# Two diffusion layers on one core: 32 products of the tile of ones by itself on TensorE, ahead of the first sums of squares

## The chip, the core and the metric

The kernel runs on one core of a Trainium2 chip. The metric is the time of one execution on the device, in microseconds (us). The engines are named as in the profile: PE is TensorE's matmul and PEld its weight load, DVE is VectorE, ACT is ScalarE, POOL is GpSimd, SP is SyncE, which here only issues DMAs.

## What is computed

Two layers of a diffusion transformer over 512 latent tokens and 256 context tokens with 1024 features, all in float32. Each layer normalises its input (root mean square), scales and shifts it by vectors made from a conditioning vector, runs attention, projects, and runs a SwiGLU feed-forward part. The part that matters here is the very beginning of layer 0:

```python
silu_c = jax.nn.silu(c)[:, None, :]
sh_a, sc_a, ... = jnp.split(silu_c @ mod_w[l] + mod_b[l], 6, axis=-1)
a_lat = rms_norm(h_lat) * (1 + sc_a) + sh_a      # modulate
p_lat = a_lat @ w_in
```

The output is the final normalisation of the latent stream, 512 by 1024.

## The kernel before, in words

Tokens lie along the free dimension and features along the 128 partitions, so x is eight tiles `X[k]` of 128 features by 512 latent and 256 context tokens. The tile `ones` (128 by 128, float32, all 1.0) is filled by DVE in line 177; it is the operand that sums over partitions.

The first stage runs as follows (lines 867 to 912).

- Lines 161 to 163 load the latent columns of the eight `X[k]`, half from SP's queue and half from POOL's.
- Lines 871 to 874 square each tile on ACT (`square_sum`, line 363) and add the squares on DVE (line 366) into one tile, `acc`.
- `first_norm` (line 796) sums `acc` over the partitions with four products by one column of `ones` (line 801), takes the root on ACT (line 803), the reciprocal on DVE (line 804) and makes a diagonal tile of it on DVE (line 805).
- `chunk(1, 0)` (line 815) makes a quarter of the scale vector: eight products of the conditioning vector by weights that SP's queue has loaded (line 823). `norm_spread` (line 809) spreads the reciprocal roots over the partitions with one product by `ones` (line 811) and copies the result into `r` (line 813). `chunk(0, 0)` makes the first quarter of the shift vector.
- `chunk_put` (line 827) copies such a quarter out (line 829), turns it with two small products (line 830) and adds the bias on DVE (line 835).
- Then `modulate` (line 409) makes `A[k]` on DVE (414), ACT (415) and DVE (416), and `start_products` (line 862) multiplies each `A[k]` by the value weights, which are loaded, cast and split on ACT and DVE in `load_start` (lines 848 and 849). Each such product is made of three (lines 757 to 759). `latent(k)` calls it for four token tiles, `context(k)` for two.

Three things set the order of the work. All products of this first stage are chained: `run` makes each group of products follow the last, so PE does them as they are written. The banks for the results come from `PM()`, which takes the PSUM tags `o` and `t` in turn; the four other tags of the first stage are held by the running sums `ov`. And the order on every engine is planned when the kernel is built: `SCHED` asks for a planner that gives each engine, at each time of a modelled run, the ready instruction with the best priority. Priorities follow the written order, and helpers shift some of them (`shifted`, for background work that makes the later scale and shift vectors, and for weights of later stages).

```python
def PM():
    turn[0] += 1
    return PS("ot"[turn[0] % 2])

def run(first, last):
    behind(first, *tip)
    tip[:] = [last]
```

After the first stage (from about 60 us on) come the projections, two attention parts, the output projection and the feed-forward part of layer 0, and the same for layer 1.

Of the kernel before, what the change touches and what calls it, by code (L numbers as in the profile page):

```python
# [14 lines left out]
P = 128  # L15
# [53 lines left out]
PATTERN = ("fbsfbsfbbsfs",) * 3  # L69
BG = ((0, 0, 0, 0, 0), (2, 3), (0, 0), (0, 0))  # L70
FIRST = 2000
STEPS = ((2, 3, 4, 4), 5, 3)
HALVES = (slice(0, 256), slice(256, 512))
SWAP8 = [(i // 16) * 16 + (i % 16 + 8) % 16 for i in range(32)]
# [24 lines left out]
def hybrid_kernel(ctx: ExitStack, tc, I, out):  # L99
# [6 lines left out]
    def T(tag, shape, dt=F32):  # L106
        count[0] += 1
        if tag not in SIZES:
            return sb.tile(shape, dt, tag=tag, name=f"{tag}_{count[0]}", bufs=BUFS.get(tag, 1))
        n = int(np.prod(shape[1:]))  # L110
        t = sb.tile([P, SIZES[tag] // (2 if dt == mybir.dt.bfloat16 else 4)], dt, tag=tag, name=f"{tag}_{count[0]}",
                    bufs=BUFS[tag])[: shape[0], :n]
        if len(shape) == 3:
            t = t.rearrange("p (a b) -> p a b", a=shape[1])
        return t
# [4 lines left out]
    def PS(tag):  # L120
        count[0] += 1
        return ps.tile([P, 512], F32, tag=tag, name=f"ps{tag}_{count[0]}", bufs=PBUFS[tag])
# [8 lines left out]
    V, S, G, PE = nc.vector, nc.scalar, nc.gpsimd, nc.tensor  # L131
# [9 lines left out]
    def behind(ins, *before):  # L141

        for x in before:
            tc.add_manual_dep(ins.ins, x.ins.name, mybir.DependencyInfo(mybir.DependencyClass.NoSync,
                              mybir.DependencyReason.DATA), reason="products in one run")
        return ins
# [29 lines left out]
    ones = T("ones", [P, P])  # L176
# [350 lines left out]
    def weighted(o, lanes):  # L527
# [13 lines left out]
        for n in range(max(len(m) for m in moving)):  # L541
            for i, (v, _, all_qs) in [*enumerate(lanes)][::-1]:
                if n < len(moving[i]):
                    kt, qs, t = moving[i][-1 - n]
                    c = slice((qs[0] - all_qs[0]) * P, (qs[-1] + 1 - all_qs[0]) * P)
                    with shifted(-FIRST):
                        ins = PE.matmul(o[64 * i : 64 * i + 64, c], v(kt), t, start=n == 0, stop=n == len(moving[i]) - 1)  # L547
# [97 lines left out]
    @contextmanager  # L645
    def shifted(by):
        tc.cur_priority += by
        yield
        tc.cur_priority -= by
# [21 lines left out]
    def attend(jobs, lag=LAG):  # L671

        todo = deque()
        outs[1] = PS("o") if PBUFS["o"] == 1 else None
        for j in jobs:
            n, units = rate[0]
            bg(int(len_jobs[0] * units) - int((len_jobs[0] - 1) * units))
            len_jobs[0] += 1
            pattern = PATTERN[phase[0]]
            sides, back, front = pattern.count("s"), todo.popleft() if len(todo) >= lag else None, True  # L680
            i = 0
            for x in pattern:
                if x == "s":
                    step((i + 1) * n // sides - i * n // sides)
                    i += 1
                elif x == "f":
                    front = front and next(j)
                elif back:
                    back = None if next(back, back) is back else back
            while front:  # L690
                front = next(j)
            if back:
                for _ in back:
                    pass
            todo.append(j)
        for j in todo:
            for _ in j:
                pass
# [88 lines left out]
# [3 lines that stand above are left out]
# [3 lines left out]
# [4 lines that stand above are left out]
# [70 lines left out]
    for comp in (0, 1):  # L867
        for v in range(2):
            MOD[0, comp, v] = T(f"mod0{comp}{v}", [P, 8])
    acc = None  # L870
    for k in range(KT):
        acc = square_sum(acc, X[k], LATS)
# [39 lines left out]
    def beside(gen):  # L912
        side_work.append(gen)
        return gen
# [80 lines left out]
    def split_pair(p):  # L995

        tag = ("b", "st")[p - 2]
        q, k = raws[2 * p - 4 : 2 * p - 2]
        how = S.copy, G.tensor_copy, V.tensor_copy
        sets.append((new_q(tag), new_k(tag)))  # L1000
        put_q(sets[p][0], None, how[RQ[p - 2]], (G, V)[RL[p - 2]])(q, slice(0, NT))
        yield
        put_k(sets[p][1], KC[1], how[RK[p - 2]])(k, slice(0, NT))
        yield
# [63 lines left out]
    def latent_operands(h):  # L1068
        p, s = divmod(h, 2)
        r, u = NOPE[s], USED[s]  # L1070
        rr = slice(32 * (h % 4), 32 * (h % 4) + 32)
        if p < 2:
            if p == 0:
                KA.append([T("st", [P, NT], F32R) for _ in range(2)])
            QA[s].append([T("st", [P, NT], F32R) for _ in range(2)])
            for t in [*(KA[s] if p == 0 else ()), *QA[s][p]] if s else ():
                (V if "z" in EV else G).memset(f(t[:32]), 0.0)
            if p == 0:
                for i in range(2):
                    V.tensor_copy(KA[s][i][ROPE[s]], KR[i][:32])  # L1080
        (ka, kc), (qa, qb) = KA[s], QA[s][p % 2]
        for x, (hi, lo) in ((kn[p], (ka, kc)), (qn[p], (qa, qb))):
            S.copy(hi[r], x[r])
            (V if "l" in EV and p < 1 else G).tensor_tensor(lo[r], x[r], f(hi[r]), op=ALU.subtract)
        for t, x in zip((qa, qb), QR[h // 4]):
            if "d" in EV:
                dma(t[ROPE[s]], x[rr])
            else:
                G.dma_start(t[ROPE[s]], x[rr])

        def scores(o, q, keys):
            q = slice(q * P, (q + 1) * P)
            PE.matmul(o, qa[u, q], ka[u, keys], start=True, stop=False)
            PE.matmul(o, qb[u, q], ka[u, keys], start=False, stop=False)
            PE.matmul(o, qa[u, q], kc[u, keys], start=False, stop=True)

        return scores
# [12 lines left out]
    def na_jobs():  # L1110
        for p in range(4):
            if p == 3:
                lower[0] = L3
            for x in ORDER[p]:
                beside(split_pair(int(x)) if x in "23" else {"n": latent_norms, "m": mla_prepare}[x]())
            rate[0] = STEPS[0][p], BG[0][p]
            if p % 2 == 0:
# [12 lines left out]
    i = 0  # L1130
# [21 lines left out]
    def mla_jobs():  # L1152
        phase[0], lower[0] = 1, LOWER
        rate[0] = STEPS[1], BG[0][4]
        ready.append(latent_operands(1))
# [392 lines left out]
    def swa_jobs():  # L1548
        for p in range(8):
            kv = p // 4  # L1550
            po = B()
            sums, mins = T("sm", [P, 6, 2]), T("sm", [P, 6, 2])
            hs = [Head(s, stacked_scores(sets[p][s], KS[kv]), keys_of(VS, kv), span, swa_bias,
                       sink_neg[:, 2 * p + s : 2 * p + s + 1], sums, mins) for s in range(2)]
            yield from pair_jobs(hs, po, False, swa_finish(p, po, sums, mins))
            OS.append(po)
# [9 lines left out]
    lower[0] = LOWER  # L1566
    rate[0] = STEPS[2], 0
    attend(swa_jobs())
# [132 lines left out]
```

## Time and profile before

| what | value |
|---|---|
| median of 3 runs | 1612.67 us (1612.62 to 1614.48) |
| the profiled execution | 1610.99 us |
| its span, from first to last instruction | 1609.1 us |
| mean granted TensorE clock | 0.988 of full speed |
| first product on PE | 14.26 us after the start of the span |
| first product of the value projection (line 757) | 24.68 us |

Times inside the trace count from the start of the span. A view of the timeline gives start, length, engine, line, operation, output and inputs, how many records are merged, and in brackets the idle time ahead and what ended it. A view by windows gives for each stretch the busy time of the engines (with the number of records), the granted clock of TensorE, the busy share of the DMA engines and GB/s. A float32 product whose operands are plain float32 shows as two records, since line 811 issues one product and has two. The lengths of neighbouring records overlap, so the pace of PE is read from the distance of the starts.

### The profile page before, as it was taken

What the parts mean: (1) busy time and instruction counts of PE and PEld (TensorE: products, weight loads), DVE (VectorE), ACT (ScalarE), POOL (GpSimd) and SP (SyncE); (2) the same over time, 40 slices, a digit from 0 to 9 for tenths busy, and PEclk for the clock granted to TensorE, in tenths of its full rate; (3) what the DMA queues carried; (4) which work ended last, traced back from release to release, by engine and by line L of the source; (5) the groups of instructions that cost most, each with busy time, mean ns of one, the idle gap of its engine ahead of it and who ended that gap; (6) DMA issues with size and microseconds to landing.
All of it is one profiled execution on the core that took longest, in us unless ns stands there. A gap on an engine that the chain in (4) does not pass through costs nothing. (4 is left out here: it accounts for less than half of the span.)

```text
span 1609.1 us, 26559 instructions
## 1 busy us (share of the span) xinstructions
PE 1541.6 (96%) x9990; PEld 1371.1 (85%) x9990; DVE 1183.8 (74%) x2380; ACT 799.0 (50%) x1616; POOL 298.6 (19%) x324
## 2 busy tenths in 40 slices
PE   5989989999999999999999998999999999999997
PEld 3777867776899999998989896877779899899997
DVE  4773878668577678796867686779877688687685
ACT  4452587677365334342423244467756544354453
POOL 0231734230011111102021212384002000000002
PEclk9999999999999999999999998999999999999999
DMA  9634232102453455536456655132005133223322
GB/s 330 226 115 157 70 122 78 40 9 74 165 200 102 152 198 182 203 121 261 170 195 214 235 206 222 66 93 77 2 17 187 38 114 126 86 99 125 87 93 84
DMA packets 76536, 214.91 MB, mean 134 GB/s; under 512 B 10196, under 2 KB 17752, under 8 KB 76408
## 3 DMA queue, kind: packets, MB, share of 16 engines
q1 hardware_dynamic: 57432, 141.67, 26.4%
q0 software_dynamic: 16240, 68.30, 12.1%
q10 hardware_dynamic: 2736, 3.26, 0.6%
q8 instruction: 78, 1.28, 0.3%
q14 instruction: 50, 0.41, 0.1%
HBM read 186.97 MB, written 23.07 MB: 131 GB/s over the span
## 5 line engine op out<-in xcount | busy, mean ns | idle before, releaser
L318 ACT CAST wh<-wr 128x1024 fp32r<-128x1024 f32 (+2 forms) x148 | 114.8, 789 | 203.8 <-DMA wr<-in_w_dn_dram 35.4
L319 DVE TENSOR_TENSOR wl<-wr,wh 128x1024 fp32r<-128x1024 f32 (+2 forms) x145 | 135.1, 938 | 84.6 <-ACT wh L318 80.7
L553 ACT ACTIVATE p<-p,sm 128x512 f32<-128x512 f32 (+3 forms) x144 | 105.0, 730 | 32.4 <-DVE sm L557 30.5
L366 POOL TENSOR_TENSOR p<-p,p 128x256 f32<-128x256 f32 (+1 forms) x33 | 31.7, 960 | 468.5 <-PE psd L332 340.2
L1342 PE MATMUL pss<-b,wh 128*128 128x384 f32 (+1 forms) x344 | 107.0, 312 | 0.6 <-ACT b L355 0.6
L1343 PE MATMUL pss<-b,wh 128*128 128x384 f32 (+1 forms) x344 | 107.2, 312 | 0.1
L227 DVE CUSTOM_DVE_ANT_0 p<-rope,cond 128x1024 bf16<-128x1024 f32 x64 | 77.3, 1224 | 40.8 <-DMA rope<-in_mod_w_dram 40.5
L1344 PE MATMUL pss<-b,wl 128*128 128x384 f32 (+1 forms) x344 | 106.1, 312 | 0.0
L331 PE MATMUL psd<-b,wh 128*128 128x512 f32 (+3 forms) x256 | 88.2, 345 | 0.0
L329 PE MATMUL psd<-b,wh 128*128 128x512 f32 (+3 forms) x216 | 78.4, 363 | 2.9 <-ACT b L493 2.5
L547 PE MATMUL pso<-ph,b 128*64 128x256 f32 (+1 forms) x384 | 77.6, 360 | 2.1 <-DVE ph L492 2.1
L332 PE MATMUL psd<-b,wl 128*128 128x512 f32 (+3 forms) x216 | 77.1, 357 | 0.1
L547 PE MATMUL pso<-pl,b 128*64 128x256 f32 (+1 forms) x384 | 76.9, 359 | 0.2 <-DVE pl L492 0.2
L222 POOL DMA_DIRECT2D rope<-in_mod_w_dram x48 | 25.5, 531 | 244.1 <-DVE mod L227 229.3
L1344 PE MATMUL pst<-b,wl 128*128 128x384 f32 (+1 forms) x224 | 69.9, 312 | 0.0
L1343 PE MATMUL pst<-b,wh 128*128 128x384 f32 (+1 forms) x224 | 69.8, 312 | 0.0
L1342 PE MATMUL pst<-b,wh 128*128 128x384 f32 (+1 forms) x224 | 69.8, 312 | 0.0
L329 PE MATMUL pss<-st,wh 128*128 128x512 f32 (+2 forms) x200 | 68.2, 341 | 1.3 <-ACT st L1144 0.9
L331 PE MATMUL pss<-b,wh 128*128 128x256 f32 (+3 forms) x211 | 68.5, 325 | 0.1
L332 PE MATMUL pss<-st,wl 128*128 128x512 f32 (+2 forms) x200 | 68.0, 341 | 0.1
L1342 PEld LDWEIGHTS pss<-b,wh 128*128 128x128 f32 x344 | 65.2, 190 | 1.1 <-ACT b L355 0.9
L1343 PEld LDWEIGHTS pss<-b,wh 128*128 128x128 f32 x344 | 65.3, 190 | 0.9 <-DVE b L356 0.7
(674 smaller groups left out, 5423.8 us busy)
## 6 DMA issues: line engine op xcount, KB each, us to landing
wr<-in_w_gu_dram SPq DMA_DIRECT2D x88, 512.0 KB, 4.0
rope<-in_mod_w_dram POOLq DMA_DIRECT2D x48, 512.0 KB, 3.8
wr<-in_w_out_dram SPq DMA_DIRECT2D x32, 512.0 KB, 3.7
wr<-in_w_dn_dram SPq DMA_DIRECT2D x64, 256.0 KB, 2.8
p<-home POOLq DMA_DIRECT2D x40, 384.0 KB, 5.6
home<-p POOLq DMA_DIRECT2D x40, 384.0 KB, 5.0
wr<-in_w_in_dram SPq DMA_DIRECT2D x21, 512.0 KB, 3.9
nb<-in_nb_dram SPq DMA_DIRECT2D x16, 384.0 KB, 3.0
```

The source lines that it names most:

```text
L227: V.tensor_tensor_reduce(out=T("p", [P, D], mybir.dt.bfloat16), in0=w, in1=cond[:, v, :], op0=ALU.mult, op1=ALU.add, scale=1.0, scalar=0.0 ...
L318: behind(S.copy(h, r), *after[:1])
L319: behind((G if eng else V).tensor_tensor(lo, r, f(h), op=ALU.subtract), *after[1:])
L329: ins = PE.matmul(o, wh[:, k], mh[:, c], start=first and k == 0, stop=False)
L331: PE.matmul(o, wh[:, k], ml[:, c], start=False, stop=False)
L332: PE.matmul(o, wl[:, k], mh[:, c], start=False, stop=last and k == n - 1)
L366: marks["add"] = (eng or V).tensor_tensor(acc[:, :n], acc[:, :n], t[:, :n], op=ALU.add)
L547: ins = PE.matmul(o[64 * i : 64 * i + 64, c], v(kt), t, start=n == 0, stop=n == len(moving[i]) - 1)
L553: S.activation(p[:, c], p[:, c], AF.Exp, bias=nm, scale=-1.0, accum_out=dn)
L1342: PE.matmul(o, wh, xh, start=first and k == 0, stop=False, skip_group_check=not first)
L1343: PE.matmul(o, wh, xl, start=False, stop=False, skip_group_check=not first)
L1344: PE.matmul(o, wl, xh, start=False, stop=k == 3, skip_group_check=not first)
```

## The change

A constant `WARM = 32`, and ahead of the first squares, one more bank from `PM()` and 32 products of `ones` by `ones` into its first 128 columns, chained by `run`. Nothing reads their result.

```diff
+WARM = 32
...
     for comp in (0, 1):
         for v in range(2):
             MOD[0, comp, v] = T(f"mod0{comp}{v}", [P, 8])
+    d = PM()
+    for i in range(WARM):
+        ins = PE.matmul(d[:, :P], ones, ones, start=True, stop=True)
+        run(ins, ins)
     acc = None
     for k in range(KT):
         acc = square_sum(acc, X[k], LATS)
```

Since `PM()` is called once more, every later bank of the first stage that came from `t` now comes from `o`, and the other way round. Since `run` chains them, the four products of line 801 follow all 32.

## The prediction

> **What bounds the kernel now.** I read the page first, then the first 25 us in order of time, then PE's busy time and clock in equal stretches.
>
> ```profile
> span 1609.1 us, 26559 instructions
> ...
> PE 1541.6 (96%) x9990; PEld 1371.1 (85%) x9990; DVE 1183.8 (74%) x2380; ACT 799.0 (50%) x1616; POOL 298.6 (19%) x324
> ```
>
> PE is busy for 96% of the span, so over the whole the kernel is bound by PE. The change lies in the one place where PE has nothing to do: the start.
>
> ```profile
> 0.89 0.17 DVE L177 MEMSET ones<- 128x128 f32 x1
> ...
> 8.73 5.47 DVE L366 TENSOR_TENSOR p<-p,p 128x512 f32<-128x512 f32 x7 [7.68 <-ACT p L363]
> ...
> 14.25 1.78 PEld L801 LDWEIGHTS pst<-ones,p 128*128 128x128 f32 x8 [14.25 <-DVE p L366]
> 14.26 1.87 PE L801 MATMUL pst<-ones,p 128*128 128x1 f32 x8 [14.26 <-DVE p L366]
> ...
> 16.05 1.93 PE L823 MATMUL pso<-st,cond_col 128*32 128x256 f32 x16
> ...
> 16.67 0.69 DVE L805 TENSOR_TENSOR p<-ident_r,sm 128x512 f32<-128x512 f32 x1
> ...
> 17.92 2.08 PE L811 MATMUL pst<-p,ones 128*128 128x512 f32 x2
> ...
> 20.35 0.64 PE L823 MATMUL pso<-ph,cond_col 128*32 128x256 f32 x2
> ...
> 20.78 0.55 PE L823 MATMUL pso<-ph,cond_col 128*32 128x256 f32 x2
> ...
> 21.16 0.38 PE L823 MATMUL pso<-ph,cond_col 128*32 128x256 f32 x2
> ...
> 22.08 0.61 PE L830 MATMUL pso<-pick,p 128*128 128x2 f32 x4
> ...
> 22.39 1.42 DVE L414 SCALAR_TENSOR_TENSOR p<-b,mod,nb 128x512 f32<-128x512 f32 x2
> ...
> 24.68 0.80 PE L757 MATMUL pss<-wh,b 128*128 128x512 f32 x1 [2.00 <-ACT b L415]
> ```
>
> PE waits 14.26 us, until DVE has added the last square at 14.20. DVE waits for the squares, and these for x, whose loads fill the DMA engines:
>
> ```profile
> 10.00:15.00 5.00, 0.74 (x4) 0.75 (x4) 3.68 (x6) 3.59 (x6) 0.00 (x0) 1.00 1.05 387
> ```
>
> A DMA share of 1.05 at 387 GB/s says that x can't come sooner, whatever PE does. From 14.26 to 22 PE itself is on the path: sums, scale quarter, spread, shift quarter, turn, then `modulate`, then the first real product at 24.68. The same operations run faster later on:
>
> ```profile
> 30.01 0.39 PE L823 MATMUL pso<-ph,cond_col 128*32 128x256 f32 x2
> ...
> 30.23 0.39 PE L823 MATMUL pso<-ph,cond_col 128*32 128x256 f32 x2
> ```
>
> ```profile
> 38.02 0.50 PE L801 MATMUL pst<-ones,p 128*128 128x1 f32 x4
> ...
> 44.10 0.59 PE L811 MATMUL pso<-p,ones 128*128 128x256 f32 x2
> ```
>
> Starts of line 823 are 0.43 us apart at 20.35 and 0.22 at 30.01. So PE runs at half speed until about 21, although the clock column of the windows says 1.00 there: it knows of no clock before the first change that it records. What changes the clock is read from PE's windows (busy us, records, clock, DMA share, GB/s), cut where the changes fall, 3.41 us each:
>
> ```profile
> 10.87:14.28 3.41, 0.02 (x1) 1.00 1.05 387
> 14.28:17.69 3.41, 3.41 (x24) 1.00 1.05 386
> 17.69:21.11 3.42, 3.42 (x18) 1.00 1.07 358
> 21.11:24.52 3.41, 1.57 (x16) 1.00 1.03 335
> 24.52:27.93 3.41, 3.25 (x8) 0.50 1.04 373
> 27.93:31.35 3.42, 3.42 (x40) 1.00 1.05 400
> ...
> 45.00:48.41 3.41, 1.34 (x5) 1.00 1.00 399
> 48.41:51.83 3.42, 3.42 (x10) 0.50 1.05 395
> ...
> 79.13:82.55 3.42, 0.34 (x2) 1.00 0.23 77
> 82.55:85.96 3.41, 2.90 (x13) 0.50 0.22 77
> 85.96:89.37 3.41, 2.06 (x15) 1.00 0.53 167
> 89.37:92.79 3.42, 1.17 (x5) 1.00 0.79 291
> 92.79:96.20 3.41, 3.41 (x10) 0.50 0.53 161
> ```
>
> The reader is to see a rule with no exception among these rows: a window in which PE was busy for 1.57 us or less is followed by one at exactly 0.50, one with 2.06 or more by one at 1.00. The early rows fit the same cuts: the speed changes between 20.78 and 21.16, at the cut 21.11. The window from 14.28, busy all along, did not raise the clock; it holds the sums, which stream one column each, and the narrow products of line 823, so busy time there isn't streaming.
>
> **The change part by part.** *Added: 32 products, two records each, 64 records.* They can start when `ones` is filled, at 0.89 + 0.17 = 1.06; I take 1.2. For the pace no row shows this product, but the nearest bound it closely. At half speed line 801 loads 8 weights in 1.78 us, 0.22 each, and line 811 streams 512 columns twice in 2.08 us: its second record is 1.22 us long, so the starts are 0.86 apart, or 0.215 for 128 columns. Load and stream of neighbours overlap in all these rows, so 0.215 a record. At full speed:
>
> ```profile
> 1089.11 0.93 PE L501 MATMUL psd<-ident_r,p 128*128 128x128 f32 x7
> ```
>
> The last of seven is 0.27 long, so (0.93 - 0.27) / 6 = 0.11 us. With the cuts of this trace (0.63, 4.04, 7.45, 10.87) the window to 4.04 is busy for 2.84 us, nearly the 2.90 that raised the clock at 85.96. Then (4.04 - 1.2) / 0.215 = 13.2 records run at half speed and 50.8 x 0.11 = 5.6 us follow: the products end at 9.6. If the clock rises only at 7.45, 29.1 records are slow and 34.9 x 0.11 = 3.8 us follow: they end at 11.3. If it never rises, 1.2 + 64 x 0.215 = 15.0.
>
> *What this does to the sums.* In the first two cases PE is free again 2.9 to 4.6 us ahead of 14.26, so the 32 cost the path nothing; DVE's chain to 14.20 is the cover. In the third the sums start 0.7 us late. And the clock: in the first case the window 10.87 to 14.28 holds no product, in the second 0.4 us, both far under 1.57. So the clock falls to half at 14.28, 0.02 us after the sums begin, and everything from there runs as before. **The gain on these cuts is nothing.**
>
> In another execution the cuts may lie otherwise; one trace cannot tell. The best place: products end at 11.3, a window that holds the last 2.06 us of them closes at 11.3 - 2.06 + 3.41 = 12.65 and keeps the clock, and the next closes at 16.06. The sums then run at full speed: 8 x 0.50 / 4 = 1.0 us instead of 1.87, 0.87 gained, and the scale quarter for the most part, so that the spread starts when the diagonal is ready, at 17.36 - 0.87 = 16.5 instead of 17.92: 1.4 gained at most. So between 0 and -1.4 us; I take -0.5.
>
> The Trainium skill (TensorE: Matmul & The Clock Gate, Seeing it yourself) prints a run in which the clock fell back 5.2 us after the last product. By that it would fall here at 9.6 + 5.2 = 14.8, and the first 0.6 us of sums would run fast, 0.3 gained, 1612.4; this trace speaks against so long a grace, as the clock fell at 24.52, under 2 us after line 830 ended at 22.08 + 0.61 = 22.69.
>
> *Moved: the banks.* `o` and `t` change places for the whole stage. `t` has two buffers, one of which is held, so both give one bank, used in turn at the same distance as before. Nothing; bounds 0.4 us either way, the 0.37 to 0.39 us of one small step.
>
> *The order on the other engines.* It is planned from modelled durations, and 32 products and a shifted clock are new to the plan. No row prices that; its ends are the rivals below.
>
> *Sum.* The profiled execution took 1610.99, its span 1609.1 and 1.9 around it; the median lies 1.7 above it. 1612.67 - 0.5 = **1612.2**. A measurement of this kernel tells about 0.2%, 3.2 us, from no change, so this is within it.
>
> **The rivals.** *1: the full clock holds (faster).* If PE still runs fast at 14.26 and on, the path shrinks: sums -0.87; spread starts 1.4 earlier in all, as above, and takes 2 x 0.59 - 0.1 = 1.1 instead of 2.08, so -2.4; the shift quarter takes 1.06 (30.01 to its last end) instead of 1.6, so -3.0. The first real product then starts near 21.7, the window to 24.52 holds 2.8 us of products, and the half window from 24.52 is spared: another 3.41 / 2 = 1.7. Together -4.7: **1608.0**. For it: the early steps all lie on the path, and after 27.93 PE is busy without a break. Against it: the empty window ahead of 14.28. It needs products that last at least to about 13, or a clock that stays up longer than at 24.52. What it may lose again is a late weight, since the DMA share is 1.03 to 1.07 up to 31 us.
>
> *2: the plan is redrawn for the worse (slower).* The place is 60 to 100 us:
>
> ```profile
> 60.00:80.00 20.00, 19.47 (x86) 15.77 (x84) 19.21 (x37) 11.11 (x22) 11.38 (x7) 1.00 0.38 129
> 80.00:100.00 20.00, 13.35 (x61) 11.53 (x62) 19.78 (x53) 12.00 (x35) 13.70 (x9) 0.83 0.44 147
> ```
>
> ```profile
> 83.06 0.55 PE L329 MATMUL pss<-b,wh 128*128 128x256 f32 x1 [3.59 <-DVE mod L253]
> ```
>
> DVE is full (19.21 and 19.78 of 20) and PE waits on it, 3.59 us at once. DVE instructions that PE needs and background ones for scale and shift vectors share that queue. Each background one (a row of line 227 gives 1.22 us) that the new plan puts ahead costs PE its length:
>
> ```profile
> L227 DVE CUSTOM_DVE_ANT_0 p<-rope,cond 128x1024 bf16<-128x1024 f32 x64 | 77.3, 1224 | 40.8 <-DMA rope<-in_mod_w_dram 40.5
> ```
>
> From three on (3.7 us) it decides. I price it at five, 6.1 us: **1618.7**. For it: the plan is one chain of choices by modelled time. Against it: if the model too has PE idle before the first sums, nothing after them moves and the order stays. The same lottery can gain as well, by about as much; a smaller chance, as PE has only 4% to win and DVE's full stretch everything to lose.
>
> *3: load and stream do not overlap.* Then a record takes 0.22 + 0.215 = 0.435 at half speed and about 0.22 at full, and the products end at 16.7 to 18.4. The sums start 2.4 to 4.1 late, but at full clock, worth -3.0: between -0.6 and +1.1, **1612.9**, again within 0.2%. L501's row, where each record has its own load and still comes every 0.11, speaks against it.
>
> **How the numbers follow.** The forecast, clock falls back and the order holds nearly: 0.39, with rival 3 at 0.04, both within 0.2%. Rival 1: 0.16, and a plan redrawn for the better: 0.08. Rival 2: 0.33. So faster 0.24, same 0.43, slower 0.33. The time is that of the likeliest, 1612.2. For 8 in 10 the range takes in rival 1 with a part of the better plans (1606.5) and most of rival 2, to about six instructions of 1.22 us (1620.0). Alone, the likeliest case reaches from 1610.9 (-1.4 and the banks) to 1613.8 (0.7 late and the banks).
>
> **What will show it.** The new line's 64 records should start by 1.3, come every 0.215 us, then every 0.11, and end between 9.5 and 11.5. The first clock change on record should be a fall close to 14.3, and the starts of line 823 near 20 us should again be 0.43 apart. The first product of line 757 (renumbered) should start within 1.4 us of 24.68. If it starts near 21.7, rival 1 is right. If the first 60 us look alike and the idle times of PE between 79 and 99 have grown, or the lines come in another order, it is rival 2. A last product after 14.3 would break the pace that I assumed.

## The result, and the profile after

| | before | changed |
|---|---|---|
| median | 1612.67 us (7 runs, 1610.09 to 1615.73) | 1618.85 us (7 runs, 1615.72 to 1621.31) |
| ratio | | 1.0038, 95% interval 1.0022 to 1.0053 |
| the profiled execution, its span, its mean clock | 1610.99, 1609.1, 0.988 | 1615.72, 1613.9, 0.982 |

The changed kernel is slower by 0.38%, some 6 us. The forecast was 1612.2, no change that can be told; the price of rival 2, 1618.7, is what came.

From the page of the changed kernel, the span and the busy time of each engine:

```profile
span 1613.9 us, 26686 instructions
...
PE 1554.7 (96%) x10054; PEld 1385.0 (86%) x10054; DVE 1182.6 (73%) x2380; ACT 799.3 (50%) x1616; POOL 300.0 (19%) x324
```

PE has 64 more records, as counted, and 13.1 us more of busy time. The new products hold 9.1 of these (next view). So the 9990 old records take 4.0 us longer than before, although they are the same products. The windows below put this down to time at half clock. PE's idle time is 59.2 instead of 67.5. At the start 9.4 us of idle went (14.26 before; 1.10 and 3.78 now), so elsewhere there is 1.1 us more. 4.0 and 1.1 make 5.1, and the span grew by 4.8. What is lost is thus clock more than waiting.

The first 25 us of PE in order of time (start, length, and in brackets the idle time ahead and what ended it):

```profile
1.10 9.10 PE L873 MATMUL pst<-ones 128*128 128x128 f32 x64 [1.10 <-DVE ones L178]
13.98 1.05 PE L802 MATMUL pso<-ones,p 128*128 128x1 f32 x8 [3.78 <-DVE p L367]
...
16.83 1.85 PE L812 MATMUL pso<-p,ones 128*128 128x512 f32 x2
18.62 0.41 PE L824 MATMUL pst<-ph,cond_col 128*32 128x256 f32 x2
...
22.82 0.79 PE L758 MATMUL pss<-wh,b 128*128 128x512 f32 x1 [2.01 <-ACT b L416]
```

The products end at 10.2. The sums take 1.05 instead of 1.87, and the first real product starts 1.86 earlier than before, at 22.82 instead of 24.68. The start is better. The windows of this execution, cut at its own clock changes (busy us with records, clock, DMA share, GB/s), show why:

```profile
8.09:11.51 3.42, 2.12 (x19) 1.00 1.04 397
11.51:14.92 3.41, 0.94 (x8) 1.00 1.05 387
14.92:18.33 3.41, 3.41 (x20) 0.50 1.05 384
18.33:21.75 3.42, 2.48 (x25) 1.00 0.93 297
21.75:25.16 3.41, 2.34 (x6) 0.50 0.87 267
25.16:28.57 3.41, 3.41 (x12) 0.50 1.01 362
```

The cuts lie 0.64 us later than before. The window that closes at 11.51 still holds 2.12 us of products and keeps the clock up until 14.92, so all the sums run at full speed. Then the clock falls, as forecast. Two more half windows follow from 21.75; the forecast's rule did not expect the second, since 2.34 us busy at half speed were followed by half again.

The loss comes later. PE's waits between 76 and 100 us (in brackets), first in the kernel before:

```profile
83.06 0.55 PE L329 MATMUL pss<-b,wh 128*128 128x256 f32 x1 [3.59 <-DVE mod L253]
88.53 0.35 PE L329 MATMUL pst<-b,wh 128*128 128x256 f32 x1 [1.10 <-DVE b L492]
91.62 0.50 PE L329 MATMUL psd<-b,wh 128*128 128x512 f32 x1 [2.49 <-ACT b L493]
```

then in the changed kernel:

```profile
80.29 0.58 PE L330 MATMUL pss<-b,wh 128*128 128x256 f32 x1 [2.52 <-ACT b L494]
88.27 0.55 PE L330 MATMUL pst<-b,wh 128*128 128x256 f32 x1 [3.59 <-DVE b L493]
91.77 0.79 PE L330 MATMUL psd<-b,wh 128*128 128x512 f32 x1 [0.81 <-ACT b L494]
```

and the windows there:

```profile
76.36:79.77 3.41, 1.41 (x7) 1.00 0.12 26
79.77:83.18 3.41, 2.89 (x13) 0.50 0.39 136
83.18:86.59 3.41, 1.50 (x13) 1.00 0.41 145
86.59:90.01 3.42, 1.74 (x8) 0.50 0.62 202
90.01:93.42 3.41, 2.60 (x9) 0.50 0.53 187
93.42:96.83 3.41, 3.41 (x9) 0.50 0.61 171
```

The waits are not longer in sum: 6.92 us against 7.18. They lie elsewhere, because PE now does some products of this stretch in another order (eight of lines 330 to 333, which ran from 98.83 us on in the kernel before, come ahead of the last wait), and so they empty other windows. Four windows run at half speed, where before there were two (from 82.55 and from 92.79). Half of the busy time in a half window is lost: (2.89 + 1.74 + 2.60 + 3.41) / 2 = 5.3 us against (2.90 + 3.41) / 2 = 3.2. In the 20 us from 80 the two kernels do as many products, 62 and 61 records, and this takes 1.96 us more of PE, at a mean clock of 0.66 instead of 0.83:

```profile
80.00:100.00 20.00, 15.31 (x62) 13.25 (x63) 19.78 (x49) 11.92 (x34) 14.04 (x9) 0.66 0.52 172
```

A second place follows near 195. No instruction changes its place there, on any engine. It has one gap of three short waits, of the same length in both kernels within 0.01 us. First the changed kernel:

```profile
193.48 0.38 PE L748 MATMUL pss<-st,st 128*128 128x256 f32 x1 [0.55 <-DVE sm L558]
194.86 0.33 PE L502 MATMUL psd<-ident_r,p 128*128 128x128 f32 x1 [0.16 <-ACT p L554]
196.03 0.53 PE L748 MATMUL pss<-st,st 128*128 128x192 f32 x1 [0.84 <-DVE sm L558]
```

Its windows:

```profile
192.41:195.83 3.42, 2.02 (x11) 1.00 0.49 122
195.83:199.24 3.41, 3.21 (x15) 0.50 0.27 58
199.24:202.65 3.41, 3.41 (x17) 0.50 0.38 115
```

and the kernel before, whose third wait ended at 196.12:

```profile
191.80:195.21 3.41, 2.66 (x17) 1.00 0.72 168
195.21:198.63 3.42, 2.57 (x23) 1.00 0.27 58
```

The same gap is divided between two windows before, 2.66 and 2.57 us busy, and the clock stays. In the changed kernel it falls mostly into one, 2.02 us busy, and the clock falls for two windows. The third wait, which starts this lag from nothing, ends at 196.03 against 196.12; 32 us on, the changed kernel is 2.98 us behind (line 962 is 967 now). In the kernel before:

```profile
227.78 2.90 PE L962 MATMUL psd<-b,ones 128*128 128x512 f32 x4 [0.61 <-DVE b L958]
```

and after:

```profile
230.76 2.90 PE L967 MATMUL psd<-b,ones 128*128 128x512 f32 x4 [1.09 <-DVE b L963]
```

A third place is from 235 to 250 us, where PE again does some products in another order. There the waits do get longer, 2.47 us against 1.19. Before:

```profile
237.35 0.39 PE L747 MATMUL pss<-b,b 128*128 128x256 f32 x1 [0.18 <-DVE sm L557]
239.77 0.33 PE L501 MATMUL pst<-ident_r,wr 128*128 128x128 f32 x1 [0.20 <-DVE pl L492]
241.94 0.36 PE L747 MATMUL pss<-b,b 128*128 128x192 f32 x1 [0.81 <-DVE sm L557]
```

and changed:

```profile
241.10 0.39 PE L748 MATMUL pss<-b,b 128*128 128x256 f32 x1 [0.53 <-DVE sm L558]
244.93 0.33 PE L502 MATMUL pst<-ident_r,wr 128*128 128x128 f32 x1 [0.90 <-DVE pl L493]
249.00 0.43 PE L548 MATMUL pso<-ph,b 128*64 128x256 f32 x1 [1.04 <-DVE ph L493]
```

### The profile page after: what moved, and what is told of

Its sections match the earlier page's. It is cut to its first block, busy times and chain, and to the rows that moved or that the text cites. A ratio compares the mean times of both kernels' runs of the same rounds, so it can differ in the third digit from the quotient of the medians.

```text
span 1613.9 us, 26686 instructions
## 1 busy us (share of the span) xinstructions
PE 1554.7 (96%) x10054; PEld 1385.0 (86%) x10054; DVE 1182.6 (73%) x2380; ACT 799.3 (50%) x1616; POOL 300.0 (19%) x324
## 5 line engine op out<-in xcount | busy, mean ns | idle before, releaser
L748 PE MATMUL pss<-st,st 128*128 128x256 f32 (+3 forms) x194 | 62.3, 340 | 5.6 <-DVE sm L558 5.4
L1347 PEld LDWEIGHTS pss<-b,wh 128*128 128x128 f32 x344 | 65.2, 190 | 1.1 <-ACT b L356 0.9
```

The lines of the kernel that those rows point to most:

```text
L748: PE.matmul(o, x, ks[0][:, keys], start=True, stop=False)
L1347: PE.matmul(o, wh, xh, start=first and k == 0, stop=False, skip_group_check=not first)
```

## The theories and what tells them apart

The order of the programs was compared engine by engine. Counted as the fewest instructions that have to be moved to turn one order into the other, the changed kernel moves 27 of the 9394 products of before on PE, 28 of 2368 instructions on DVE, 17 of 1430 on ACT, 6 of 414 on SP and none on POOL. (An expectation that names twice as many counts each in both orders.) Two edits make this, each without the other. The one extra call of `PM()`, with no product at all, moves 14 on PE: six that run from 62.8 us on in the kernel before, and eight that run from 98.8 us on. The 32 products with the bank count put back (`turn[0] += 1` behind them) move 13 others, 11 of them between 236 and 250 us. Between 109 and 233 us nothing moves on any engine. 24 products with the bank count put back move nothing at all, and every buffer stays where it was.

**Theory 1**: the redrawn order costs the time, and the products do nothing bad. **Theory 2**: the products themselves cost it on the chip, by their work or by the clock that they change. **Theory 3**: the losses hang on where the windows of the clock happen to fall in an execution, so they come and go by chance. What an expectation says of the clock at the start is the prediction's rival 1.

## The experiments

All but e8 were timed in five rounds against the kernel before on the same chip. e1 to e4 share 35 runs of it (median 1613.74), e5 to e7 22 (1613.25), e9 to e12 29 (1613.52). All edits stand at the place of the change, in the kernel before.

**e1, the extra bank alone.**

```diff
+    d = PM()
```

> No products at all, only the one more call of PM() that makes the banks o and t change places (the output stays as it was). The plan of this kernel differs from before only in two places of PE's order, around 49 and 80 us, and in DVE's order around 80 to 100 us. Theory 1 (the plan is what costs): in the changed kernel PE stood 1.7 us ahead of before at 78 us and level with it at 99 us, so this plan alone should cost about 1.7 us in the stretch from 78 to 99 us, and nothing at 195 us: 1614.4. Theory 2 (the products on the chip cost, by their clock or their reads): without products nothing changes, 1612.7. Theory 3 (the losses hang on where the clock's windows fall, by chance): 1612.7 as well, with half windows in other places from run to run.

Measured: 1617.6 us, ratio 1.0024, interval 1.0014 to 1.0034. **e11** is the same kernel again.

> The bank flip alone again. Theory 1 (order): 1616 to 1618, with a step of 0.7 to 2.1 us between 78 and 100 us; the steps of its first trace near 195 and 840 us, if they are chance, need not be there again. If the first result was chance: 1613 to 1614.

Measured: 1617.24, ratio 1.0026, interval 1.0015 to 1.0036. One call that gives out a bank and adds no instruction costs 4 us. That is more than theory 1's 1614.4, which counted on no loss near 195 us; e1's trace has one there (table below). Theory 3 fails as pure chance: the cost came back in 11 further executions on another chip, and the step at 80 us with it. In e11's trace the waits between 76 and 100 are those of the changed kernel:

```profile
80.45 0.51 PE L330 MATMUL pss<-b,wh 128*128 128x256 f32 x1 [2.51 <-ACT b L494]
88.45 0.55 PE L330 MATMUL pst<-b,wh 128*128 128x256 f32 x1 [3.37 <-DVE b L493]
91.94 0.79 PE L330 MATMUL psd<-b,wh 128*128 128x512 f32 x1 [0.81 <-ACT b L494]
```

**e2, 24 products and the bank count put back**: products on the chip, order of before.

```diff
+WARM = 24
...
+    d = PM()
+    for i in range(WARM):
+        ins = PE.matmul(d[:, :P], ones, ones, start=True, stop=True)
+        run(ins, ins)
+    turn[0] += 1
```

> 24 products of ones by ones, and the banks left as before (PM's turn is set back), so that every engine has the very order of before. Only what the products do on the chip is left. Theory 1: nothing is lost, and the early gain of the changed kernel (up to 1.7 us at 78 us) stays if the clock is still up at 14 us, which 24 products make less likely than 32, since they end near 8.5 us: 1611.0 to 1612.7. Theory 2: the loss is there, 1618.9, or three quarters of it, 1617.3. Theory 3: about 1612.7, with half windows moved.

Measured: 1612.27, ratio 0.9997, interval 0.9987 to 1.0007. The waits of before are back, with 3.60, 1.14 and 2.49 us:

```profile
82.94 0.55 PE L330 MATMUL pss<-b,wh 128*128 128x256 f32 x1 [3.60 <-DVE mod L254]
88.42 0.36 PE L330 MATMUL pst<-b,wh 128*128 128x256 f32 x1 [1.14 <-DVE b L493]
91.50 0.51 PE L330 MATMUL psd<-b,wh 128*128 128x512 f32 x1 [2.49 <-ACT b L494]
```

**e7, 64 products and the bank count put back** (as e2, `WARM = 64`). On PE the order is that of before; one instruction moves on DVE, one on ACT and five on SP.

> 64 products, banks as before: PE's order is that of before, and those of DVE, ACT and SP differ in a handful of places. The products end near 17.2 us, so the sums start about 2.9 us late, but at full clock, which shortens the path to the first product by 3.0 us, and the half window at 24.5 us may be spared (1.7 us). Theory 1: 1611 to 1614. Theory 2: 1625, the loss twice as large as with 32.

Measured: 1613.07, ratio 0.9996, interval 0.9984 to 1.0009. Twice as many products as the change cost nothing, though they make the sums late:

```profile
1.10 16.74 PE L873 MATMUL pst<-ones 128*128 128x128 f32 x128 [1.10 <-DVE ones L178]
...
17.68 0.95 PE L802 MATMUL pst<-ones,p 128*128 128x1 f32 x8
...
25.24 0.50 PE L758 MATMUL pss<-wh,b 128*128 128x512 f32 x1 [2.01 <-ACT b L416]
```

The sums start 3.4 us later than before, the first real product 0.56 us later: the full clock from 14 to 25 us is worth 2.9 us, as the prediction's rival 3 had counted (3.0). e2 and e7 speak against theory 2.

**e3, 32 products and the bank count put back** (as e2, `WARM = 32`): the other half of the redrawn order.

> All 32 products, the banks left as before. The plan differs from before at 195 to 205 us and near 400 us on PE, and not at 49 and 80 us. Theory 1: the early gain is kept past 99 us (-1.7), and the step of +3.4 us at 195 to 260 us that the changed kernel shows is there, with its later small ones (+1.4): 1615.8. Theory 2: the whole loss, 1618.9. Theory 3: the step at 195 us comes only if a window of the clock closes in a gap there; about 1611 to 1614.

Measured: 1617.01, ratio 1.0028, interval 1.0013 to 1.0042. This half costs 3.3 us in the medians by itself, 1.2 more than theory 1's sum.

**e4, 24 products, bank not put back** (as e2, without its last line). Its order is that of e1, instruction for instruction.

> 24 products with the one more bank, so the plan of e1 with products on the chip. Theory 1: like e1 with an early gain of 0 to 1.7 us: 1612.7 to 1614.4. Theory 2: 1617.3 to 1618.9. Theory 3: about 1612.7. Against e1 it tells what products do on the chip under the same plan, a second time beside e2 against before.

Measured: 1613.14, ratio 1.0006, interval 0.9997 to 1.0015. **e12** is the same again.

> 24 products in the flipped bank again, whose order is that of the bank flip alone. Theory 1: within 1 us of the bank flip run beside it, both above the kernel before by 1 to 4 us. If the 24 products gain what the flip costs: 2 to 3 us below the bank flip alone again, at 1613 to 1614.5, and the trace's lead must then be gained ahead of 78 us.

Measured: 1615.88, ratio 1.0015, interval 1.0002 to 1.0027. Less than e1 and e11 both times, with the same order, by 4.5 and 1.4 us in the medians; so e12 came out between its two expectations. The intervals of e11 and e12 overlap, those of e1 and e4 hardly. Of e4's executions 8 of 11 took under 1615 us, of e1's 2 of 11. This is not settled (below).

**e5, the changed kernel again.**

> The changed kernel once more, unaltered, beside the others on one chip: a second trace and more runs. Theory 1 (plan): 1617 to 1620, and the trace again loses about 1.6 us between 78 and 99 us, where its plan differs. Theory 3 (chance of the clock's windows): the steps at 195 and 840 us of the first trace need not be there again.

Measured: 1618.22, ratio 1.0030, interval 1.0011 to 1.0049.

**e6, 40 products in the changed kernel** (`WARM = 40`), with exactly its order.

> 40 products in place of 32: every engine has the very order of the changed kernel, but the products end near 12.0 us, 1.8 us later, so that the clock is still full for the sums and most of the scale quarter wherever its windows fall. Theory 1: as slow as the changed kernel, less 0 to 1 us: 1617.5 to 1619. Theory 2 (the products themselves cost): a quarter more loss, 1620.4. If the clock at the start were what decides (the rival 1 of the prediction), clearly faster than 32: 1614 or less.

Measured: 1620.56, ratio 1.0050, interval 1.0030 to 1.0069. The clock stayed full until 16.7 us, and the sums ran in 1.05 us from 13.94. A start at full clock did not make it faster. The time is also what theory 2 gave, 1620.4. But its interval takes in the ratio of the changed kernel itself (1.0038), and e7, above, has 24 products more and no loss.

**e8, the kernel before once more**, for a second trace: how far two traces of one kernel differ.

> The kernel before, unaltered, for a second trace. Theory 1: between 60 and 100 us the waits of PE are those of the first trace (3.6, 1.1 and 2.5 us), with two half windows. Theory 3: half windows elsewhere, near 195 or 840 us, can appear here too; then those steps of the changed kernel's trace are chance, and not its plan.

Measured: 1613.29 (one run). From 78 to 250 us its distance from the first trace changes by no more than 0.1 us (table below), so it shows no loss near 195; near 840 it has one of 1.6 us.

**e9, 32 products of one column**: nearly the order of the changed kernel (2 instructions differ on PE, 4 on DVE), but hardly any streaming.

```diff
+WARM = 32
...
+    d = PM()
+    for i in range(WARM):
+        ins = PE.matmul(d[:, :1], ones, ones[:, :1], start=True, stop=True)
+        run(ins, ins)
```

> 32 products of which one column moves instead of 128, into the same extra bank: the order is nearly that of the changed kernel (on PE four instructions differ), but PE hardly streams at the start, so the clock should fall as before the change. Theory 1 (the redrawn order costs the time, its two parts being the bank and the 32 products in the plan): as slow as the changed kernel and without its early gain of 1 to 1.7 us, 1617 to 1620; the step between 78 and 100 us of 0.7 to 2.1 us is there. Theory 2 (the loss comes from the streaming of the products or the clock that they raise): 1612.5 to 1613.7, no step there.

Measured: 1619.58, ratio 1.0038, interval 1.0023 to 1.0053. As slow as the change at its first measurement, without its streaming.

**e10, the same with the bank count put back** (`turn[0] += 1` behind): 11 moved instructions on PE.

> The same 32 narrow products with the bank count put back: the 32 products' part of the redrawn order alone, without streaming. Theory 1: 1615 to 1617 (the changed kernel with old banks gave 1617.0 with an early gain of about 1 us), no step between 78 and 100 us and one of 0.4 to 3.2 us between 205 and 262 us. Theory 2: 1612.5 to 1613.7, no steps.

Measured: 1617.17, ratio 1.0025, interval 1.0014 to 1.0037; with the same half of the order, e3 gave 1.0028. Between 76 and 100 its PE waits are those of before, and past 200 it has a half window that before has not:

```profile
207.05:210.46 3.41, 1.61 (x9) 0.99 0.53 160
210.46:213.87 3.41, 3.41 (x20) 0.51 0.58 171
```

**The places in all traces.** The table gives how far the same product of PE lies behind the first trace of before (us; single traces). The bank half of the order moves products of PE within the step from 78 to 100, the products' half within that from 235 to 250; within that from 194 to 224 nothing moves. The column behind the steps gives PE's busy time in the emptier of the windows that hold the gap near 195, and the clock of the next window; in the first trace of before these are 2.57 and full.

| kernel | moved order | at 28 | at 78 | step 78 to 100 | step 194 to 224 | step 235 to 250 | window near 195 | ratio of the times |
|---|---|---|---|---|---|---|---|---|
| changed | both | -1.7 | -1.7 | +1.6 | +3.1 | +1.1 | 2.02, half | 1.0038 |
| e5 | both | -1.7 | -0.9 | +1.7 | +4.5 | +1.1 | 1.91, half | 1.0030 |
| e6 | both | -1.4 | -0.9 | +2.1 | +3.0 | +1.6 | 1.88, half | 1.0050 |
| e9 | both | -0.2 | -0.9 | +1.9 | +6.1 | +1.3 | 1.80, half | 1.0038 |
| e1 | bank | -0.2 | -0.2 | +2.1 | +1.2 | 0.0 | 1.81, half | 1.0024 |
| e11 | bank | -0.8 | -1.5 | +1.9 | +3.0 | 0.0 | 1.80, half | 1.0026 |
| e4 | bank | 0.6 | 0.8 | +0.7 | 0.0 | 0.0 | 2.48, full | 1.0006 |
| e12 | bank | -0.7 | -0.7 | +2.0 | +1.3 | 0.0 | 1.81, half | 1.0015 |
| e3 | products | -2.2 | -0.8 | 0.0 | +1.5 | +1.0 | 2.36, half | 1.0028 |
| e10 | products | 1.1 | 1.2 | -1.6 | +3.9 | +1.4 | 2.36, half | 1.0025 |
| e2 | none | -0.2 | -0.1 | 0.0 | 0.0 | 0.0 | 2.58, full | 0.9997 |
| e7 | none on PE | 0.5 | 1.9 | 0.0 | 0.0 | 0.0 | 2.57, full | 0.9996 |
| e8 | none | -0.2 | -0.6 | 0.0 | 0.0 | 0.0 | 2.57, full | (before) |

The step at 78 to 100 is there in all eight traces with the bank half and in none of the five without it (e10 gains 1.6 there, with the waits of before and fewer half windows). The step at 235 to 250 is +1.0 to +1.6 in all six with the products' half, and 0.0 in the seven without it. The step near 195 came in nine of the ten traces with a moved order, whichever half it was. The ratios say the same with all their runs: two halves cost 0.30 to 0.50%, one half 0.06 to 0.28%, none nothing. The three steps together make 5.8 us in the changed kernel's trace, 3.3 in e1's and 2.5 in e3's; the medians moved by 6.2, 3.9 and 3.3. Behind 262 us single traces tell nothing of the order: up to the end, e8 falls another 3 us behind the first trace and e2 nearly 7, with the order of before.

## Why the prediction was wrong, step by step

- **The new products: right.** 64 records, start at 1.10. With this execution's cut at 4.68 the prediction's paces give (4.68 - 1.10) / 0.215 = 16.7 slow ones and 47.3 x 0.11 = 5.2 us, so 9.9, and 10.2 with the length of the last. They ended at 10.2. One reading behind the pace was wrong: of line 811's two records the first is 1.22 us long and the second 1.06, so their starts are 1.02 apart and not 0.86. The pace of 0.215 stood all the same: line 801's starts give it, and the new records came every 0.213 at half clock.
- **The clock at the start: right in kind, small in size.** It fell before the narrow products of line 824, at 14.92, 4.7 us after the last new product. This is not the first change on record, which is the rise at 4.68. The gain was bounded at 1.4 us and was 1.86, since the spread (16.83), too, brought the next rise forward, from 21.11 to 18.33. But it does not last. At 28 us, kernels with 32 or 40 streaming products lead by 1.4 to 2.2; at 78 by 0.8 to 1.7, where e11, without any product, leads by 1.5. In the median nothing of it is seen: the change 1.0038 and 1.0030, e9 without streaming 1.0038.
- **"Moved: the banks. Nothing; bounds 0.4 us either way": failed.** On the chip the change of banks by itself cost nothing that shows: up to 78 us e1 and e11 are not behind before (-0.2 and -1.5). (Beside `o` and `t`, only the tags `s` and `d` are in use there: `ov` holds these and one of the two buffers of `t`.) But the banks' tags are an input to the planner, and one changed tag redraws the order from 61 to 108 us: e1 and e11, 4 us.
- **"The clock falls back and the order holds nearly", 0.39, and with it the sum's zero for the order: failed, and this is the step that decided.** The term was put at nothing and measured about 6 us: 24 products in the old order cost nothing (e2, 0.9997), the order of the bank half without any product costs 3.9 us (e1), and nearly the whole order with narrow products 6.1 (e9). No row of before prices it, as the prediction says; a comparison of the two orders would have shown at once that the order does not hold.
- **Rival 2: right in sign and in time, wrong in its working.** Its 6.1 us were five instructions of 1.22 us put ahead on DVE between 60 and 100 us. There, the changed kernel loses only 1.6, by half clock windows and not by longer waits. The larger part is lost near 195 (3.1) and from 235 to 250 (1.1), places that no rival named; only in the last do longer waits for DVE, the rival's mechanism, make the loss. That the two prices agree is luck. Its sign in the profile did show, as the lines near 80 us come in another order. What it said against itself, "if the model too has PE idle before the first sums, nothing after them moves", overlooked the banks: in e1 nothing is put on PE and the order moves. For the products it held with 24 (e2) and not with 32 (e3).
- **Rival 1**: its full clock was there in e6 (until 16.7 us) and in e7, without its gain. e7 paid for it with late sums. e6, with the changed order, lost it.
- **The rule for the windows** (1.57 us or less: half; 2.06 or more: full) held for the rows of before that the prediction shows, but for the one from 14.28 that it excepts. It did not hold after: 2.34 and 2.60 at half speed were followed by half, and so was 2.36 at full speed in e3 and e10. 2.02, between its two bounds, was followed by half as well. Busy time is a rough measure of what the gate, which sets the clock, counts.

**What stays open.** Near 195 the waits are the same in all 14 traces, and no instruction moves; the clock falls where the emptier window holds 1.80 to 2.36 us of busy time and stays where it holds 2.48 or more. So the loss there hangs on where the window's cut lies. Counted at the same product, it lies from 194.97 to 195.21 us in the four traces with PE's order of before, at 194.85 in e4, from 195.92 to 196.49 in the seven others with the bank half, and at 194.38 and 193.83 in e3 and e10. It is thus not free to fall anywhere in the 3.41 us of a window, as theory 3 would have it. That the moved order of earlier stretches sets it is likely, but argued and not shown. Why 24 products with e1's order cost less than e1 (1.0006 and 1.0015 against 1.0024 and 1.0026) is not explained. e4's trace loses only 0.7 us at 80 and nothing near 195, since its cut lies as in the kernel before, but e12's loses as e1's does; and their sums ran at half speed as in e1 (1.87 us in e12). The intervals are too wide to add the halves: 4 and 3.3 us would make 7, and the whole gave 5 to 7. A redrawn order also puts buffers elsewhere, and the runs hardly part the two: only e7, with PE's order of before, has 640 products on other buffers, and it lost nothing. A further step of 2.1 us near 840 in the changed kernel's trace looks like chance, since e8 has one of 1.6 there too.

## What to carry to other kernels

In a kernel whose order a planner makes, an edit, even of the tag of a buffer, can change two things, the work and the order; before a price is put on the work, compare the emitted order with the old one on every engine. To tell them apart, run the order without the work (e1, and e9 nearly) and the work with the old order (e2, and e7 nearly). A gain of 1 to 2 us at the start is not worth a redrawn order that costs 5 to 7 us, as both halves did here; of these variants, those that keep the order (e2, e7) are within 0.1% of the kernel before.

## What the runs showed of the hardware

- Three waits of 0.55, 0.16 and 0.84 us, some 1.55 us together, closed the clock gate (the clock fell to half) for two windows of 3.41 us when they fell mostly into one window (2.02 us busy), and not when they were divided so that each of two windows was fuller (2.66 and 2.57). Over 14 traces, 1.80 to 2.36 us busy here closed it for one window or two, and 2.48 or more did not; elsewhere at full clock 2.06 and 2.12 us did not close it either, so busy time alone doesn't tell. The Trainium skill (TensorE: Matmul & The Clock Gate, Why this matters for your kernels) advises to avoid idle gaps of over about 3 us; here far shorter ones did it, and the measurement decides.
- Being busy is not enough to raise the clock. In e9, 64 records that load 128 columns of weights and stream one came every 0.215 us, as many as at half speed with 128 streamed columns. PE is busy without a break, and the clock rose only at 19.73, at the end of the window that holds most of the spread. The first row is from the order of time, and the others are e9's windows; their 1.00 ahead of 19.73 stands for "no change on record yet":

```profile
1.10 13.81 PE L873 MATMUL pst<-ones 128*128 128x1 f32 x64 [1.10 <-DVE ones L178]
14.78 1.84 PE L802 MATMUL pso<-ones,p 128*128 128x1 f32 x8
```

```profile
9.49:12.90 3.41, 3.41 (x18) 1.00 1.05 390
12.90:16.32 3.42, 3.42 (x18) 1.00 1.05 386
16.32:19.73 3.41, 3.41 (x20) 1.00 1.07 374
```

The sums' 1.84 us, against 1.05 in the changed kernel, show that the clock was at half.
